# Memory attention of the first layer two steps earlier, its value products in the banks of the turned tiles, filler products given out at five rates

## The chip, the cores and the metric

The kernel runs on one core of a Trainium2 chip. TensorE (PE in the profile; its weight loads are PEld) multiplies matrices into PSUM, which holds eight banks of 128 rows by 512 float32. ScalarE (ACT), VectorE (DVE) and GpSimd (POOL) do the rest, and SyncE (SP) issues most transfers. The metric is the device time of one execution in microseconds (us), and less is better. Every engine works through its own list of instructions in the order in which the program gives them, and an instruction that must wait for another engine waits on a semaphore.

## The reference

One batch of 512 tokens of width 1024 goes through two layers. The first layer mixes tokens by differential attention (six heads, each with two maps of 64 columns), the second by gated linear attention. In every layer, in parallel with that, four heads of cross-attention read 256 memory tokens. A gated MLP with a causal convolution follows. What matters here is the first layer:

```python
proj = h @ w_in_diff[j]                 # queries, keys, values of 6 heads; queries of the memory attention
mix = diff_attention(q, k, v, ...)      # 6 heads x 4 blocks of 128 queries, softmax of two maps, p0 - lam * p1
...
# memory_cross_attention(mem_q, mem, mem_norm[i], w_mem_kv[i], mem_qk_norm[i])
kv = rms_norm(mem, mem_norm_g) @ w_kv
logits = jnp.einsum('bqhd,bkhd->bhqk', q, k)
p = jax.nn.softmax(logits, axis=-1)
o = jnp.einsum('bhqk,bkhd->bqhd', p, v)
...
x = x + jnp.concatenate([mix, cross], axis=-1) @ w_out[i]
```

## The kernel before

Large products are done in split precision: each operand is a high part (rounded to fp32r) and a low part, and three matmuls of 128x512 stand for one product (hi·hi, hi·lo, lo·hi). A block of weights comes by DMA as `raw`; `split_weights` makes `whi` on ACT (line 201) and `wlo` on DVE (line 204). `whi` and `wlo` have five buffers each (`WB`), so a new cast waits until TensorE has used the block that lay in its buffer.

The order on TensorE is the order in which the program is written (its schedule is manual). ACT, DVE, POOL and SP are ordered by a planner that works with its own estimates of durations. So moving a TensorE step also changes the order of the other engines' lists around it.

`diff_layer` is a loop of 28 steps, t = 0 to 27. Unit u = 0 to 23 is head u // 4, block u % 4. Step t does, in this order:

1. `logits(t)`: scores of unit t into two banks of the pair `lg` (line 604); DVE adds the bias and takes the row bound (line 609), ACT takes the exponentials (line 612), and DVE combines the two maps (lines 615 to 618).
2. `values(t-2)`: the value products of unit t-2 into the head's bank of the pair `sm` (line 640). At a head's last block ACT squares (line 645), and DVE scales the result out of the bank as `o` (line 649).
3. a first share of filler, `F.fill(f)`.
4. now and then norms, and `keys0()` at one step: the memory keys are transposed and scaled into `kmT` (line 473).
5. `turn(t-1)`: unit t-1's weights are transposed into a bank of the pair `tp` (line 170) and copied out by ACT (line 629).
6. the memory attention's part of the step, with m = t - M0: `ma.turn(m-1)` (bank of `tp`; copied out by DVE for even numbers and by ACT for odd ones, line 524), `ma.values` at m = 3, 5, 7, 9 (line 537, bank of `sm`), `ma.logits` at m = 0, 2, 4, 6 (line 504, banks of `lg`; DVE line 507, ACT line 511).
7. a second share of filler.
8. `prepare` of two heads at t = 7, 8, 15, 16 (queries and keys of the head transposed into two banks of `tp` and scaled by ACT, line 580), and `finish` of a head at t = 7, 11, 15 and so on (`o` transposed into a bank of `tp`, split by ACT line 238 and DVE line 239).

Each of the pairs `mm`, `sm`, `lg`, `tp` has two banks; together they are all eight. A bank is written again when the engine that reads it has finished.

The filler (class `Filler`) is a queue of product pieces: the second and third heads' projections, memory keys and values of both layers, and from step 16 the output projection. A piece of 512 columns is six matmuls; it is entered at 1.296 us. `F.fill(us)` adds credit and gives out pieces until the credit is used; an overdraft is carried on. `F.need(name)` gives out everything up to a mark.

The profile's times belong to steps like this: TensorE starts `logits` of step 5 at 82.97 us, of 6 at 90.67, 8 at 109.17, 12 at 147.31, 13 at 156.53, 15 at 173.56, 16 at 181.82, 17 at 190.43, 18 at 197.39, 22 at 217.60.

Of the kernel before, what the change touches and what calls it, by code (L numbers as in the profile page):

```python
# [30 lines left out]
HALVES = (6, 5)  # L31
XS = 36
WB = 5
STEPS, FILL = (14, 20, 26), (2.9, 1.2, 0.8, 1.3)
K8 = tuple(range(KT))
C4 = tuple(range(4))

# [92 lines left out]
def trunk(ctx, tc, head_d, x_t, mem_t, wpack, cols_a_d, cols_d, conv_d, gate_d, rel_bias, diff_lambda, consts, onehot, out):  # L130
# [12 lines left out]
    def bank(tag):  # L143
        return ps.tile([128, 512], F32, name=f"ps_{tag}", tag=tag)
# [4 lines left out]
    def split_tiles(pool=None, tag="xs", bufs=XS):  # L149
        pool = pool or xs  # L150
        return (pool.tile([128, S], F32R, name=tag + "h", tag=tag, bufs=bufs),
                pool.tile([128, S], F32R, name=tag + "l", tag=tag, bufs=bufs))
# [4 lines left out]
    def blk(b, w=128):  # L157
        return slice(w * b, w * b + w)
# [78 lines left out]
    def split(hi, lo, src, gain):  # L237
        A.activation(hi, src, AF.Copy, scale=gain)
        V.scalar_tensor_tensor(lo, src, gain, hi.bitcast(F32), op0=ALU.mult, op1=ALU.subtract)  # L239
# [4 lines left out]
    def gemm(sh, sl, nb, key, w, evac, hook=None):  # L244
        got, open_ = [], {}

        def unit(b, k0, k1):
            if not got:
                got.extend(weights(key))
            if k0 == 0:  # L250
                open_[b] = bank("mm")[:, :w]
            p = open_[b]
            for k in range(k0, k1):
                hi, lo = got[k]
                mm(p, sh[k][:, blk(b)], hi, start=k == 0, stop=False)  # L255
                mm(p, sh[k][:, blk(b)], lo, start=False, stop=False)  # L256
                mm(p, sl[k][:, blk(b)], hi, start=False, stop=k == KT - 1)  # L257
            if k1 == KT:
                if hook is not None and b == 0:
                    hook()  # L260
                evac(b, open_.pop(b))
        for b in range(nb):
            for k in range(0, KT, 2):
                F.add(6 * w / 2370.0, lambda b=b, k=k: unit(b, k, k + 2))
# [183 lines left out]
    def mem_kv(l):  # L448
        hs, ls = [None] * KT, [None] * KT
        km = [None]  # L450

        def operands():
            if l == 0:
                mem_squares()
            km[0] = xtile().rearrange("p (b n) -> p b n", b=2)
            for k in range(KT):
                if k % 2 == 0:
                    mh, ml = split_tiles()
                c = blk(k % 2, 256)
                hs[k], ls[k] = mh[:, c], ml[:, c]  # L460
                split(hs[k], ls[k], memT[k // 2][:, c], c_mem(l, k))

        def ev(b, p):
            A.activation(km[0][:, b], p[:, :256], AF.Copy, scale=r_mem[:, b:b + 1])
            A.activation(vm[l][:, b], p[:, 256:], AF.Copy, scale=r_mem[:, b:b + 1])

        def keys():
            F.need(f"kv{l}")
            p = bank("lg")
            for hp in range(2):  # L470
                for b in range(2):
                    transpose(p[:, 256 * hp + 128 * b:256 * hp + 128 * b + 128], km[0][:, b, blk(hp)])
            A.activation(kmT[l].rearrange("p a b -> p (a b)"), p, AF.Copy, scale=c_mk(l))
        gemm(hs, ls, 2, ("kv", l), 512, ev,
             (lambda: token_rsqrt("lg", mem_acc[0], 2, r_mem)) if l == 0 else None)
        F.add(0.0, lambda: group_norm(None, km[0], 2, 4, 64))
        F.mark(f"kv{l}")
        return operands, keys


    class MemAttn:
# [46 lines left out]
        def values(self, b):  # L528
            if b == 0:
                for hp in range(2):  # L530
                    self.mix[6 + hp] = split_tiles()
            pT = self.live.pop(2 * b), self.live.pop(2 * b + 1)
            po = bank("sm")
            for hp in range(2):
                for kb in range(2):
                    for j in range(2):
                        mm(po[blk(j, 64), blk(hp)], vm[self.l][:, kb, blk(2 * hp + j, 64)],
                           pT[j][:, blk(2 * hp + kb)], start=kb == 0, stop=kb == 1)
            for hp in range(2):
                mh, ml = self.mix[6 + hp]  # L540
                split(mh[:, blk(b)], ml[:, blk(b)], po[:, blk(hp)], 1.0)
# [3 lines left out]
    def diff_layer(pool, mix, acc):  # L545
# [14 lines left out]
        def project_qk(pr):  # L560
            qk[pr] = (pool.tile([128, NB, 256], F32, name="qs", bufs=1),
                      pool.tile([128, NB, 256], F32, name="ks", bufs=1))
            gemm(xh, xl, NB, ("qk", pr), 512, halves(*qk[pr]))
            F.mark(f"qk{pr}")
# [3 lines left out]
        def norms(pr, i):  # L568
            F.need(f"qk{pr}")
            group_norm(pool, qk[pr][i], NB, 4, 64)  # L570
# [51 lines left out]
        def turn(u):  # L622
            i = u % 4
            nk = 128 * (i + 1)
            pt = bank("tp")
            for kb in range(i + 1):
                transpose(pt[:, blk(kb)], live[u][:, blk(kb)])
            wT = xtile()
            A.copy(wT[:, :nk], pt[:, :nk])
            live[u] = wT  # L630
# [40 lines left out]
        F.fill(1.2)  # L671
        prepare(1)
        ma = MemAttn(pool, 0, qm, mix, False)
        M0 = 10
        for t in range(28):
            if t == 0:
                project_qk(1)
                ops0, keys0 = mem_kv(0)
                gemm(xh, xl, NB, ("v", 1), 512, lambda b, p: A.activation(
                    v12[:, b], p, AF.Copy, scale=r[:, b:b + 1]))  # L680
                F.mark("v1")
                project_qk(2)
            if t == 2:
                ops0()
                ma.norm()
            if t == 12:
                ops1, keys1 = mem_kv(1)
                ops1()
            if t == 22:
                keys1()  # L690
            if t == 16:
                load_x(x_t)
                out_proj(0, mix, 0, None)
            if t == 26:
                rest = out_proj(0, mix, 1, acc, 5)
            f = FILL[bisect(STEPS, t)]
            m = t - M0
            if t < 24:
                logits(t)
            if 0 <= t - 2 < 24:  # L700
                values(t - 2)
            F.fill(f)
            if t in (5, 6, 13, 14):
                norms((t + 3) // 8, (t + 3) % 8)
            if t == 9:
                keys0()
            if 0 <= t - 1 < 24:
                turn(t - 1)
            if 1 <= m < 9:
                ma.turn(m - 1)  # L710
            if m in (3, 5, 7, 9):
                ma.values(m // 2 - 1)
            if m in (0, 2, 4, 6):
                ma.logits(m // 2)
            if t == 27:
                F.flush()
            F.fill(f)
            if t == 4:
                ma.queries()
            if t in (7, 8, 15, 16):  # L720
                prepare(2 * (t // 7) + (t + 1) % 8)
            if t % 4 == 3 and t >= 7:
                finish(t // 4 - 1)
# [248 lines left out]
    def load_x(src):  # L972
        for k in range(KT):
            xT[k] = xtile()
            nc.sync.dma_start(xT[k], src[k])
# [10 lines left out]
    def out_proj(l, mix, part, acc, late=None):  # L986
        got, kk = {}, dict(PASS[l][part])
        turns = cycle(("mm", "mm", "sm", "sm") if late is not None else ("mm", "sm") if acc else ("mm",))

        def unit(n, i):  # L990
            c, ks = n // 2, kk[n // 2]
            if i == 0:
                if c not in got:
                    got[c] = weights(("o", l, part, c))
                got["p", n] = bank(next(turns))
            p = got["p", n]
            product(p, got[c], n % 2, [mix[k] for k in ks], (i,))
            if i == len(ks) - 1:
                update(n, p, None if acc is None else (lambda k: c_ffn(l, k)), acc)

        def give(units):
            for u in units:
                F.add(0.65, lambda u=u: unit(*u))
        units = [(2 * c + n, i) for c, ks in PASS[l][part] for n in range(2) for i in range(len(ks))]
        if late is None:
            return give(units)
        early = [u for u in units if u[0] < 4 and kk[u[0] // 2][u[1]] != late]
        give([u for u in early if u[0] < 3])
        return lambda: give([u for u in early if u[0] == 3] + [u for u in units if u not in early])
# [158 lines left out]
```

## Time and profile before

| what | value |
|---|---|
| median of 3 runs | 1196.5 us (1195.61 to 1196.85) |
| the profiled execution | 1194.47 us |
| its span | 1192.7 us |
| TensorE busy | 1179.3 us (99%) |
| VectorE busy | 760.1 us (64%) |
| ScalarE busy | 548.3 us (46%) |
| GpSimd busy | 4.5 us |
| mean transfer rate | 99 GB/s |

TensorE is nearly always busy, so time can be won or lost only in the gaps between its instructions, or by giving it more or fewer of them. Its matmuls overlap: a 128x512 matmul is shown with about 0.39 us, but the next starts 0.23 us later. In a row of the timeline the first number is the start, the second the duration, and brackets show the idle time before it with what ended it.

### The profile page before, as it was taken

To read this page: it belongs to the slowest core of one execution; us is meant where nothing else is said; L and a number is where in the kernel's file an instruction comes from. 1 tells how busy PE (TensorE), PEld (TensorE's weight loads), DVE (VectorE), ACT (ScalarE), POOL (GpSimd) and SP (SyncE) were. 2 spreads that over 40 slices of the span, in tenths; PEclk is the share of its full clock that TensorE was granted. 3 is DMA by queue.
4 is the path that set the end of the run, shared out by engine and by line. 5 is a ranking of instruction groups with operands and counts; after the bars stand their busy time and mean duration, and the time that the engine had idled before them with its cause. 6 is when DMAs were issued, how large, how long until landed. Compare 5 with 4: busy or idle time off the path is not lost.

```text
span 1192.7 us, 14774 instructions
## 1 busy us (share of the span) xinstructions
PE 1179.3 (99%) x5656; PEld 965.8 (81%) x5656; DVE 760.1 (64%) x1270; ACT 548.3 (46%) x966; POOL 4.5 (0%) x25
## 2 busy tenths in 40 slices
PE   9999998999999999999999999999999999999998
PEld 6887776788888888888888788987888888888887
DVE  7566587687767434767556746768777743476741
ACT  6676586564434223434436534436443422243420
POOL 0000000000000000000000000000000000000000
PEclk9999999999999999999999999999999999999999
DMA  8322214042322332322342221333233233242231
GB/s 296 124 96 81 80 55 141 27 136 76 116 96 86 109 107 71 123 71 89 117 144 78 72 71 58 103 104 125 73 109 103 81 114 106 71 124 72 89 115 44
DMA packets 39268, 117.81 MB, mean 99 GB/s; under 512 B 4671, under 2 KB 6520, under 8 KB 39198
## 3 DMA queue, kind: packets, MB, share of 16 engines
q1 hardware_dynamic: 39054, 116.62, 30.5%
q8 instruction: 44, 0.72, 0.3%
q10 hardware_dynamic: 144, 0.26, 0.1%
q14 instruction: 26, 0.21, 0.1%
HBM read 112.65 MB, written 4.21 MB: 98 GB/s over the span
## 4 chain that ended last, share of the span: by engine, by line
PE 93%; DVE 3%; ACT 2%; DMA 1%; issue 1%; SPq 0%; ACTq 0%; DVEq 0%
PE ps_mm L273 8%; PE ps_mm L274 8%; PE ps_mm L272 8%; PE ps_sm L274 7%; PE ps_sm L273 7%; PE ps_sm L272 7%; PE ps_mm L255 5%; PE ps_mm L257 5%; PE ps_mm L256 5%; PE ps_lg L273 3%; PE ps_lg L272 3%; PE ps_lg L274 3%; PE ps_tp L272 3%; PE ps_tp L273 3%; PE ps_tp L274 3%; PE ps_tp L170 2%
## 5 line engine op out<-in xcount | busy, mean ns | idle before, releaser
L201 ACT CAST whi<-raw 128x1024 fp32r<-128x1024 f32 (+4 forms) x212 | 208.5, 985 | 263.9 <-PE ps_tp L273 134.7
L204 DVE TENSOR_TENSOR wlo<-raw,whi 128x1024 fp32r<-128x1024 f32 (+4 forms) x212 | 241.3, 1140 | 117.1 <-ACT whi L201 116.4
L272 PE MATMUL ps_mm<-xsh,whi 128*128 128x512 f32 x446 | 176.4, 396 | 0.0
L273 PE MATMUL ps_mm<-xsl,whi 128*128 128x512 f32 x446 | 173.8, 390 | 0.2 <-DVE xsl L239 0.2
L274 PE MATMUL ps_mm<-xsh,wlo 128*128 128x512 f32 x446 | 173.7, 389 | 0.0
L272 PE MATMUL ps_sm<-xsh,whi 128*128 128x512 f32 x386 | 150.3, 389 | 0.0
L274 PE MATMUL ps_sm<-xsh,wlo 128*128 128x512 f32 x386 | 150.2, 389 | 0.0
L273 PE MATMUL ps_sm<-xsl,whi 128*128 128x512 f32 x386 | 150.2, 389 | 0.0
L255 PE MATMUL ps_mm<-whi,xsh 128*128 128x512 f32 (+2 forms) x352 | 136.9, 389 | 0.1
L257 PE MATMUL ps_mm<-whi,xsl 128*128 128x512 f32 (+2 forms) x352 | 131.1, 373 | 0.3 <-DVE xsl L239 0.3
L256 PE MATMUL ps_mm<-wlo,xsh 128*128 128x512 f32 (+2 forms) x352 | 130.6, 371 | 0.0
L1028 ACT ACTIVATE cvo<-u,cv 128x512 f32<-128x512 f32 x88 | 71.6, 814 | 121.4 <-DVE u L1026 121.4
L273 PEld LDWEIGHTS ps_mm<-xsl,whi 128*128 128x128 f32 x446 | 83.8, 188 | 17.8 <-DVE xsl L239 0.6
L272 PEld LDWEIGHTS ps_mm<-xsh,whi 128*128 128x128 f32 x446 | 83.8, 188 | 17.5 <-issue 0.8
L274 PEld LDWEIGHTS ps_mm<-xsh,wlo 128*128 128x128 f32 x446 | 83.7, 188 | 17.4
L1029 DVE SCALAR_TENSOR_TENSOR cvo<-u,cv,cvo 128x512 f32<-128x512 f32 x88 | 65.8, 748 | 38.7 <-ACT cvo L1028 38.7
L273 PEld LDWEIGHTS ps_sm<-xsl,whi 128*128 128x128 f32 x386 | 72.5, 188 | 15.1
L272 PEld LDWEIGHTS ps_sm<-xsh,whi 128*128 128x128 f32 x386 | 72.5, 188 | 15.0
L274 PEld LDWEIGHTS ps_sm<-xsh,wlo 128*128 128x128 f32 x386 | 72.5, 188 | 15.0
L255 PEld LDWEIGHTS ps_mm<-whi,xsh 128*128 128x128 f32 x352 | 66.3, 188 | 13.8 <-issue 3.4
L257 PEld LDWEIGHTS ps_mm<-whi,xsl 128*128 128x128 f32 x352 | 66.1, 188 | 12.6 <-DVE xsl L239 0.5
L256 PEld LDWEIGHTS ps_mm<-wlo,xsh 128*128 128x128 f32 x352 | 66.4, 189 | 9.7
(257 smaller groups left out, 1734.9 us busy)
## 6 DMA issues: line engine op xcount, KB each, us to landing
raw<-in_wpack_dram SPq DMA_DIRECT2D x178, 512.0 KB, 3.5
xt<-in_x_t_dram SPq DMA_DIRECT2D x15, 256.0 KB, 5.9
raw<-in_wpack_dram SPq DMA_DIRECT2D x15, 256.0 KB, 2.6
raw<-in_wpack_dram SPq DMA_DIRECT2D x8, 384.0 KB, 3.4
xres<-xt SPq DMA_DIRECT2D x8, 256.0 KB, 2.0
xt<-xres SPq DMA_DIRECT2D x8, 256.0 KB, 3.9
out_dram<-xt SPq DMA_DIRECT2D x8, 256.0 KB, 2.0
bt<-bias_d SPq DMA_DIRECT2D x6, 256.0 KB, 3.1
```

What stands on the lines that cost most here:

```text
L170: nc.tensor.transpose(dst, src, ident[:n, :n])
L201: ins = A.copy(hi[:, c], raw[:, c])
L204: V.tensor_sub(lo[:, c], raw[:, c], hi[:, c].bitcast(F32))
L255: mm(p, sh[k][:, blk(b)], hi, start=k == 0, stop=False)
L256: mm(p, sh[k][:, blk(b)], lo, start=False, stop=False)
L257: mm(p, sl[k][:, blk(b)], hi, start=False, stop=k == KT - 1)
L272: mm(p, hi[:, blk(n)], bh, start=i == first, stop=False)
L273: mm(p, hi[:, blk(n)], bl, start=False, stop=False)
L274: mm(p, lo[:, blk(n)], bh, start=False, stop=i == last)
L1028: A.activation(c, u[:, 2:], AF.Identity, scale=cv[l][:, 2, j:j + 1], bias=cv[l][:, 3, j:j + 1])
L1029: V.scalar_tensor_tensor(c, u[:, 1:S + 1], cv[l][:, 1, j:j + 1], c, op0=ALU.mult, op1=ALU.add)
```

## The change

- `M0` goes from 10 to 8: all four `ma.logits`, the eight `ma.turn` and the four `ma.values` of the first layer are issued two steps earlier (steps 8 to 17 where they were in 10 to 19).
- `keys0()` moves from the middle of step 9 to the end of step 7.
- In the first layer `ma.values` writes a bank of the pair `tp` where it wrote one of `sm`.
- The four split tiles of the memory attention's result (`mix[6]`, `mix[7]`) come from a pool of their own with four buffers, where they took four of the 36 buffers `xs`.
- The filler's credits are five where they were four: 3.2 us for steps 0 to 7, 2.5 for 8 to 13, and then 1.2, 0.8 and 1.3 as before; it was 2.9 for steps 0 to 13.

```diff
-STEPS, FILL = (14, 20, 26), (2.9, 1.2, 0.8, 1.3)
+STEPS, FILL = (8, 14, 20, 26), (3.2, 2.5, 1.2, 0.8, 1.3)
...
         def values(self, b):
             if b == 0:
                 for hp in range(2):
-                    self.mix[6 + hp] = split_tiles()
+                    self.mix[6 + hp] = split_tiles() if self.l else split_tiles(self.pool, "mx", 4)
             pT = self.live.pop(2 * b), self.live.pop(2 * b + 1)
-            po = bank("sm")
+            po = bank("sm" if self.l else "tp")
...
-        M0 = 10
+        M0 = 8
...
             F.fill(f)
             if t in (5, 6, 13, 14):
                 norms((t + 3) // 8, (t + 3) % 8)
-            if t == 9:
-                keys0()
             if 0 <= t - 1 < 24:
                 turn(t - 1)
...
             F.fill(f)
             if t == 4:
                 ma.queries()
+            if t == 7:
+                keys0()
             if t in (7, 8, 15, 16):
                 prepare(2 * (t // 7) + (t + 1) % 8)
```

The number of instructions is the same. In the changed program TensorE's list differs from step 1 to step 19, in the order of the filler pieces and of the memory attention, and in tile names in the output projection; the lists of ACT and DVE are reordered by the planner between steps 1 and 20. GpSimd's list is the same. On SP's queue one weight load of 512 KB is issued ahead of a bias load instead of behind it.

## The prediction

> **What bounds the kernel now.** First the head of the page, then the busy time in stretches of 10 us (columns: stretch; busy us and instructions of PE, PEld, DVE, ACT, POOL; granted clock; share and rate of the DMA).
>
> ```profile
> span 1192.7 us, 14774 instructions
> PE 1179.3 (99%) x5656; PEld 965.8 (81%) x5656; DVE 760.1 (64%) x1270; ACT 548.3 (46%) x966; POOL 4.5 (0%) x25
> ```
>
> ```profile
> 110.00:120.00 10.00, 10.00 (x62) 8.42 (x61) 3.05 (x14) 4.91 (x15) 0.00 (x0) 1.00 0.01 2
> ...
> 170.00:180.00 10.00, 9.10 (x63) 6.52 (x62) 9.17 (x27) 7.96 (x24) 0.00 (x0) 1.00 0.10 33
> 180.00:190.00 10.00, 8.31 (x54) 6.48 (x53) 5.63 (x15) 5.67 (x16) 0.14 (x1) 1.00 0.76 265
> 190.00:200.00 10.00, 8.09 (x62) 6.14 (x60) 7.85 (x23) 8.82 (x32) 0.00 (x0) 1.00 0.21 67
> ```
>
> TensorE is the bound, at full clock. The change adds no instruction, so it can only open or close gaps on TensorE. They lie in steps 15 to 18 (170 to 200 us), where filler is scarce; at 110 us TensorE has none and DVE is two thirds idle. Next, who TensorE waited for in steps 5 to 25 (us in total, times, longest), and the timeline rows of the waits that matter.
>
> ```profile
> PE ps_sm L640 <- DVE o L649: 2.2, 1, 2.2
> PE ps_lg L504 <- DVE nmd L609: 1.3, 1, 1.3
> PE ps_lg L604 <- ACT xt L511: 1.1, 3, 0.5
> ...
> PE ps_lg L604 <- ACT kmT L473: 0.4, 1, 0.4
> ```
>
> ```profile
> 60.37 0.39 PE L256 MATMUL ps_mm<-wlo,xsh 128*128 128x512 f32 x1
> 60.60 0.40 PE L257 MATMUL ps_mm<-whi,xsl 128*128 128x512 f32 x1
> ...
> 90.67 1.61 PE L604 MATMUL ps_lg<-kT,qT 64*128 64x192 f32 x8
> ...
> 126.45 0.92 PE L604 MATMUL ps_lg<-kT,qT 64*128 64x192 f32 x8
> ...
> 162.54 0.71 PE L170 MATMUL ps_tp<-C,xt 128*128 128x128 f32 x5
> 163.18 1.09 PE L537 MATMUL ps_sm<-xt,vm 128*64 128x128 f32 x16
> ...
> 178.62 1.09 PE L537 MATMUL ps_sm<-xt,vm 128*64 128x128 f32 x16
> 179.64 0.55 PE L170 MATMUL ps_tp<-C,qs 128*128 128x128 f32 x3
> 180.13 0.60 PE L170 MATMUL ps_tp<-C,ks 128*128 128x128 f32 x4
> 181.08 0.66 PE L170 MATMUL ps_tp<-C,o 128*128 128x128 f32 x4 [0.34 <-ACT qT L580]
> ...
> 186.70 1.34 PE L504 MATMUL ps_lg<-kmT,xt 64*128 64x256 f32 x8 [1.26 <-DVE nmd L609]
> ...
> 200.53 0.46 PE L640 MATMUL ps_sm<-v,xt 128*128 128x128 f32 x2 [2.22 <-DVE o L649]
> ```
>
> The reader is to see four things. A filler matmul costs 0.23 us (60.37 to 60.60). At step 18 head 4 waits 2.22 us for a bank of `sm` that head 3's `o` still holds, because a memory value product holds the other. At step 16 the fourth memory logits wait 1.26 us for `lg`. And at step 6 a wait hides in a busy row: eight rows take 1.61 us where the same eight take 0.92 at step 10, so 0.69.
>
> Then ACT and DVE around steps 6, 13, 15 and 16:
>
> ```profile
> 88.71 0.29 ACT L629 COPY xt<-ps_tp 128x128 f32<-128x128 f32 x1
> ...
> 95.79 1.05 ACT L201 CAST whi<-raw 128x1024 fp32r<-128x1024 f32 x1
> ...
> 163.14 0.45 ACT L556 ACTIVATE qs<-ps_mm,r_x 128x256 f32<-128x256 f32 x1
> 163.50 0.46 ACT L557 ACTIVATE ks<-ps_mm,r_x 128x256 f32<-128x256 f32 x1
> 163.86 0.62 ACT L308 ACTIVATE xt<-qs 128x512 f32<-128x512 f32 x1
> 164.38 0.25 ACT L629 COPY xt<-ps_tp 128x128 f32<-128x128 f32 x1
> ...
> 178.33 0.46 ACT L629 COPY xt<-ps_tp 128x384 f32<-128x384 f32 x1
> ...
> 180.34 0.69 ACT L580 ACTIVATE qT<-ps_tp,cols 128x512 f32<-128x512 f32 x1 [0.30 <-PE ps_tp L170]
> ...
> 184.60 0.84 ACT L201 CAST whi<-raw 128x768 fp32r<-128x768 f32 x1 [2.15 <-PE ps_mm L257]
> 185.34 0.58 ACT L629 COPY xt<-ps_tp 128x512 f32<-128x512 f32 x1
> 186.68 0.40 ACT L612 ACTIVATE xt<-xt,nmd 128x128 f32<-128x128 f32 x1 [0.76 <-DVE nmd L609]
> ...
> 187.47 0.56 ACT L524 COPY xt<-ps_tp 128x512 f32<-128x512 f32 x1
> ```
>
> ```profile
> 185.48 0.96 DVE L204 TENSOR_TENSOR wlo<-raw,whi 128x768 fp32r<-128x768 f32 x1 [2.24 <-ACT whi L201]
> 186.35 0.28 DVE L609 CUSTOM_DVE_ANT_0 xt<-ps_lg,bt 128x128 f32<-128x128 f32 x1
> ```
>
> A cast of weights (184.60) stands idle for 2.15 us until TensorE has used up the block in its buffer, and everything behind it in ACT's list stands too: the copy of the turned weights at 185.34, and through DVE's line 204 the row bounds at 186.35. Lags: ACT starts 0.15 us after TensorE's last transpose (179.64 + 0.55 to 180.34), TensorE 0.05 after ACT's end (180.34 + 0.69 to 181.08).
>
> **The change part by part.** I walked the changed program's four lists and put these durations on them. Where a number is a bound I say so.
>
> *Value products leave `sm` (gain).* Only heads use `sm` then, head 4 gets the bank that head 2 freed at step 12, and its first product waits only for its own copied weights, long done. Gain 2.22; if the copy were late, 0.
>
> *No memory logits at step 16 (gain).* The 1.26 at step 16 goes, with 0.22 at step 17 (the rest of the 1.1 of line 511; 0.9 lies at step 15 and stays, since memory logits still stand at step 14 ahead of the same two filler pieces). But that work was also cover; see step 16.
>
> *Memory attention from step 8.* The analogue of 0.22 now falls at step 9, where two pieces and eight transposes stand between memory logits and the next scores: +0.2, between 0 and 0.5. `keys0` ahead of `prepare` puts one ACT scaling in front of the head's: +0.15, between 0 and 0.4. No filler is removed, and DVE has room there (3.05 of 10 at 110 us), so steps 8, 10 and 12 cost nothing more; if that cover is gone it is 0.5 a step.
>
> *Credits.* 16 shares of 3.2 and 12 of 2.5 are 81.2 us, as 28 of 2.9 are: no filler is gained or lost, but pieces come earlier. At step 6 this moves the copy of unit 4's weights. It ran at 88.71, ahead of three casts; now it stands behind three casts and two squares. From the transpose: six matmuls until the first buffer is free, 1.4; the memory norm ahead of it, 0.5 (estimate); three casts at 0.95 (1.05 each, the next starting 0.1 before the end), 2.85; a key evacuation 0.36, two squares at 0.52, the copy 0.25, lags 0.2: 6.6. TensorE has 18 matmuls and one set of scores, 4.15 + 0.95 = 5.1. Wait 1.5, against 0.69 that goes since the memory norm now has 18 matmuls of cover: +0.8, between -0.7 (the copy in time) and +1.3.
>
> *Value products enter `tp` (loss).* Each follows at once behind `turn` and `ma.turn`, which hold both banks, so it waits for ACT's copy of `turn`. Steps 11 and 15: the copy of three blocks ends at 178.79 while the product started at 178.62: +0.3 each, between 0 and 0.7. Step 17 has no `ma.turn`: 0. Step 13: the copy stands behind the last piece's evacuation. From that piece's end: 0.15, lines 556 and 557 0.72, two squares 1.04, two small operations 0.3 (estimate), the copy 0.25, 0.05: 2.5, and TensorE arrives after 0.64 (162.54 to 163.18). Wait 1.9; the lower bound is the old run's own copy, 164.63 + 0.05 - 163.18 = 1.5; the upper 2.4, if a cast is late by half its length.
>
> *Step 15, behind the product.* `qs`, `ks` and `o` follow with the product's bank still held by its splits, so all three pass through one bank. `ks` waits for the scaling of `qs`: 0.15 + 0.69 + 0.05 = 0.9; `o` for the product's last low part: 0.3 (estimate); the old 0.34 goes. +0.85, between 0 and 1.4.
>
> [...]
>
> *Step 16 (loss).* ACT's list holds two casts of 768 columns ahead of the copy of unit 15's weights. The second waits for the last filler matmul, and right behind that matmul TensorE wants the copy's bank for `qs`. Wait 0.15 + 0.74 (184.60 to 185.34) + 0.58 + 0.05 = 1.5. `ks` then wants the bank of `ma.turn`, copied by line 524, which stands where it did at 187.47, behind the cast, line 204, the row bounds and two exponentials: 184.60 to 188.03 is 3.43 after the cast's start, so 3.63 after the filler; less 1.5 and 0.49 of `qs`, 1.6. Together 3.1, between 0.8 (cast done early, one copy left) and 3.9. In the old order memory logits stood between.
>
> *The rest.* The four tiles leave `xs`: no instruction, nothing that waited for `xs` on TensorE: 0. Their memory is used again by the MLP's `u`, whose clearing now waits until nearly the end of the output projection:
>
> ```profile
> POOL u L1015 <- PE ps_tp L170: 200.2, 2, 140.7
> ```
>
> It had 140 us of slack; the first convolution comes over 24 matmuls (5.5 us) after, so 0; without this cover a clearing of under 1 us. On SP one weight load passes a bias load; it is issued a step ahead: 0, at worst the load's landing of 3.1 us. The 0.4 at step 22 stays.
>
> ```profile
> bt<-bias_d SPq DMA_DIRECT2D x6, 256.0 KB, 3.1
> ```
>
> Sum: -2.22 - 1.26 - 0.22 + 0.2 + 0.15 + 0.8 + 0.3 + 0.3 + 1.9 + 0.85 + 3.1 = +3.9. The profiled execution took 1194.47 us, 2.0 below the median, and would be 1198.4; the median 1196.5 becomes 1200.4.
>
> **The rivals.** *ACT comes in time (faster).* If ACT reaches the copies of steps 13 and 16 within 0.64 us of their transposes, 1.9 and 3.1 shrink to 0.3 and 0; the wait of step 6 must shrink too. 3.9 - 1.6 - 3.1 - 1.5 = -2.3, and with step 15's line down to 0, -3.2: 1193.3. For it: ACT is idle by half over the span. Against: at step 16 the cast is tied to TensorE's own last matmul, and no idle time beforehand helps. It decides if the cast stands ahead of that filler on the chip.
>
> *Waits feed on each other (no change).* Each wait lets ACT and DVE catch up, so that one of the two large ones fades: 3.9 - 1.9 = +2.0, 1198.5. For it: DVE and ACT are busy 9.17 and 7.96 of 10 at 170 us, so backlog is real. Against: the two waits hang on instructions issued just before, not on backlog.
>
> *The clock falls (slower still).* Step 16 would hold TensorE for 3.1 us with 0.49 between. If the clock were halved for as long, half of it is lost again: 1202. The stretch with 2.22 idle shows 1.00, so there is no sign of it. [...]
>
> **How the numbers follow.** 0.2% (2.4 us) is about what a measurement of this kernel can tell from no change. The sum holds: 0.70. Waits fade: 0.18. In time: 0.09. Clock: 0.03. So slower 0.73, same 0.18, faster 0.09. Predicted 1200.4. All lower ends at once give -2.1, all upper ends +7.6: 1194.4 to 1204.1. I cut the lower end at 1195.8, which leaves out most of the faster case, and keep 1204.1.
>
> **What would show it.** No wait on `o` at step 18, none of line 504 at step 16; instead line 537 waiting for line 629 at step 13, about 1.9, and `qs` and `ks` waiting for lines 629 and 524 at step 16, about 1.5 and 1.6; line 640 waiting at step 6. It is wrong if line 537 starts right behind its transposes, or if step 16's copies end before the filler.

## The result, and the profile after

The changed kernel takes 1199.72 us (median of 12 runs, 1197.45 to 1202.32), the kernel before 1195.92 us in the same comparison (median of 12, 1194.44 to 1196.85). The ratio is 1.0034, with a 95% interval of 1.0024 to 1.0043: slower, by about 0.3%. The profiled execution of the changed kernel took 1197.67 us, 3.2 more than the profiled one before.

The head of its page:

```profile
span 1195.9 us, 14770 instructions
PE 1178.8 (99%) x5656; PEld 964.5 (81%) x5656; DVE 761.1 (64%) x1270; ACT 548.3 (46%) x966; POOL 4.5 (0%) x25
```

TensorE's work is what it was (1178.8 against 1179.3 us busy), and the span is 3.2 us longer: the loss is idle time. Who TensorE waited for between 80 and 240 us (us in total, times, longest):

```profile
PE ps_tp L537 <- ACT xt L629: 2.5, 3, 2.1
PE ps_tp L170 <- ACT xt L524: 1.4, 1, 1.4
PE ps_tp L170 <- ACT xt L629: 1.4, 1, 1.4
PE ps_tp L170 <- ACT qT L580: 1.3, 2, 0.8
PE ps_sm L640 <- ACT xt L629: 1.3, 1, 1.3
...
PE ps_lg L504 <- DVE nmd L609: 0.3, 1, 0.3
PE ps_lg L604 <- ACT xt L511: 0.2, 1, 0.2
```

The 2.2 for `o` is gone and the 1.3 for `nmd` is down to 0.3. In their place stand four entries of waits for ScalarE's copies of turned tiles, lines 629 and 524. TensorE's timeline says where (start, duration, idle time before it):

```profile
97.05 0.49 PE L640 MATMUL ps_sm<-v,xt 128*128 128x128 f32 x2 [1.25 <-ACT xt L629]
...
115.34 0.66 PE L170 MATMUL ps_tp<-C,o 128*128 128x128 f32 x4 [0.48 <-ACT qT L580]
...
123.94 1.06 PE L604 MATMUL ps_lg<-kT,qT 64*128 64x128 f32 x8
...
170.15 1.09 PE L537 MATMUL ps_tp<-xt,vm 128*64 128x128 f32 x16 [2.13 <-ACT xt L629]
...
181.39 1.13 PE L604 MATMUL ps_lg<-kT,qT 64*128 64x256 f32 x6 [0.21 <-ACT xt L511]
...
185.50 1.09 PE L537 MATMUL ps_tp<-xt,vm 128*64 128x128 f32 x16 [0.18 <-ACT xt L629]
...
187.96 0.66 PE L170 MATMUL ps_tp<-C,ks 128*128 128x128 f32 x4 [0.78 <-ACT qT L580]
...
195.81 0.66 PE L170 MATMUL ps_tp<-C,qs 128*128 128x128 f32 x4 [1.41 <-ACT xt L629]
197.91 0.66 PE L170 MATMUL ps_tp<-C,ks 128*128 128x128 f32 x4 [1.44 <-ACT xt L524]
...
205.19 0.49 PE L640 MATMUL ps_sm<-v,xt 128*128 128x128 f32 x2
```

The last row is head 4's first value product, without a wait. Step 6 (97.05), step 13 (170.15) and step 16 (195.81, 197.91) pay. ScalarE's rows say why:

```profile
92.50 1.04 ACT L201 CAST whi<-raw 128x1024 fp32r<-128x1024 f32 x1
...
95.27 1.04 ACT L201 CAST whi<-raw 128x1024 fp32r<-128x1024 f32 x1
96.21 0.63 ACT L308 ACTIVATE xt<-qs 128x512 f32<-128x512 f32 x1
96.74 0.26 ACT L629 COPY xt<-ps_tp 128x128 f32<-128x128 f32 x1
...
168.34 0.47 ACT L557 ACTIVATE ks<-ps_mm,r_x 128x256 f32<-128x256 f32 x1
168.70 0.21 ACT L192 ACTIVATE rs_y<-rs_y 128x4 f32<-128x4 f32 x1
168.79 1.15 ACT L308 ACTIVATE xt<-qs 128x512 f32<-128x512 f32 x2
169.83 0.27 ACT L629 COPY xt<-ps_tp 128x128 f32<-128x128 f32 x1
...
192.18 0.83 ACT L201 CAST whi<-raw 128x768 fp32r<-128x768 f32 x1 [2.19 <-PE ps_mm L257]
194.44 0.83 ACT L201 CAST whi<-raw 128x768 fp32r<-128x768 f32 x1 [1.43 <-PE ps_mm L257]
195.18 0.58 ACT L629 COPY xt<-ps_tp 128x512 f32<-128x512 f32 x1
...
197.29 0.56 ACT L524 COPY xt<-ps_tp 128x512 f32<-128x512 f32 x1
```

A copy of 0.26 to 0.58 us stands last in a row of casts and squares. At step 16 it is worse than being last: ScalarE is idle for 2.19 and 1.43 us in front of two casts, because it takes its list in order and the casts must wait for TensorE's own filler; the finished transposes wait behind. In stretches of 10 us (columns as in the prediction):

```profile
110.00:120.00 10.00, 9.52 (x55) 7.77 (x54) 2.28 (x9) 4.10 (x9) 0.14 (x1) 1.00 0.01 4
170.00:180.00 10.00, 9.85 (x64) 7.38 (x64) 9.37 (x25) 6.03 (x19) 0.00 (x0) 1.00 0.24 83
...
190.00:200.00 10.00, 7.15 (x49) 5.72 (x49) 4.64 (x14) 5.06 (x11) 0.00 (x0) 1.00 0.87 307
```

From 190 to 200 us TensorE, VectorE and ScalarE are all less busy than before (7.15, 4.64 and 5.06 against 8.09, 7.85 and 8.82): none of the three is overloaded in this stretch.

The 12 runs fall into groups by their mean granted clock: four with 1.000 lie at 1197.45 to 1197.76 (the profiled execution is one of them), three with 0.999 at 1199.44 to 1199.89, and five with 0.995 to 0.997 at 1200.73 to 1202.32; the experiments show what this is.

### The profile page after: what moved, and what is told of

It reads as the page before. It is cut to its first block, busy times and chain, and to the rows that moved or that the text cites. A ratio compares the mean times of both kernels' runs of the same rounds, so it can differ in the third digit from the quotient of the medians.

```text
span 1195.9 us, 14770 instructions
## 1 busy us (share of the span) xinstructions
PE 1178.8 (99%) x5656; PEld 964.5 (81%) x5656; DVE 761.1 (64%) x1270; ACT 548.3 (46%) x966; POOL 4.5 (0%) x25
## 4 chain that ended last, share of the span: by engine, by line
PE 90%; ACT 4%; DVE 3%; DMA 2%; issue 1%; SPq 0%; ACTq 0%; DVEq 0%
PE ps_mm L273 8%; PE ps_mm L274 8%; PE ps_mm L272 8%; PE ps_sm L273 7%; PE ps_sm L272 7%; PE ps_sm L274 7%; PE ps_mm L255 5%; PE ps_mm L257 5%; PE ps_mm L256 5%; PE ps_lg L273 3%; PE ps_lg L272 3%; PE ps_lg L274 3%; PE ps_tp L272 3%; PE ps_tp L273 3%; PE ps_tp L274 3%; PE ps_tp L170 2%
## 5 line engine op out<-in xcount | busy, mean ns | idle before, releaser
L272 PE MATMUL ps_mm<-xsh,whi 128*128 128x512 f32 x438 | 173.3, 396 | 0.0
L273 PE MATMUL ps_mm<-xsl,whi 128*128 128x512 f32 x438 | 170.6, 390 | 0.2 <-DVE xsl L239 0.2
L274 PE MATMUL ps_mm<-xsh,wlo 128*128 128x512 f32 x438 | 170.6, 390 | 0.0
L272 PE MATMUL ps_sm<-xsh,whi 128*128 128x512 f32 x378 | 147.1, 389 | 0.0
L274 PE MATMUL ps_sm<-xsh,wlo 128*128 128x512 f32 x378 | 147.1, 389 | 0.0
L273 PE MATMUL ps_sm<-xsl,whi 128*128 128x512 f32 x378 | 147.0, 389 | 0.0
```

Of the source, the lines that this page charges most:

```text
L272: mm(p, hi[:, blk(n)], bh, start=i == first, stop=False)
L273: mm(p, hi[:, blk(n)], bl, start=False, stop=False)
L274: mm(p, lo[:, blk(n)], bh, start=False, stop=i == last)
```

## The experiments

The theory is that the loss comes from ScalarE's list: copies of `tp` banks stand behind casts of weights that needn't be there. The rivals are that the bank of the value products, the rates or the earlier memory attention as such is the cause, or that the engines are just behind. Each time below is the median of the version's runs, with the ratio to the kernel before and its interval. "Undisturbed" is the median of those of its runs whose mean clock was 1.000: 1197.70 for the changed kernel (4 runs), and 1194.9 for the kernel before (39 of the 80 runs taken beside the experiments).

**The head's preparation one step later.**

```diff
-            if t in (7, 8, 15, 16):
+            if t in (7, 8, 15):
                 prepare(2 * (t // 7) + (t + 1) % 8)
...
+            if t == 17:
+                prepare(5)
```

> The changed kernel with the preparation of the head of unit 5 moved from the end of step 16 to the end of step 17; nothing else. Theory (the copies of turned tiles stand behind two casts in ScalarE's list, and the transposes of qs and ks come right behind the filler that the second cast waits for): the two waits of step 16, 1.41 for line 629 and 1.44 for line 524, go, since at step 17 a last memory value product and the scores of the step lie between; of their 2.85 us at most 0.9 comes back as a wait for qT, line 580, at step 17, so the span is 2.0 to 2.9 us below the changed kernel's. Rival 1 (ScalarE and VectorE are simply behind here, and TensorE pays wherever it next needs them): the 2.85 comes back within two steps under another name, the span is within 0.5 us of the changed kernel's. Rival 2 (memory attention was the cover that is missing, so any place without it costs the same): the waits appear at step 17 at about 1.4 each.

Measured: 1199.33 us, 1.0028 (1.0018 to 1.0038); only two of its 8 runs were undisturbed (1197.75 and 1199.11). The two waits of step 16 went, and TensorE paid elsewhere (timeline):

```profile
198.10 0.98 PE L604 MATMUL ps_lg<-kT,qT 64*128 64x128 f32 x8 [2.12 <-DVE nmd L609]
...
206.74 0.63 PE L170 MATMUL ps_tp<-C,ks 128*128 128x128 f32 x4 [0.51 <-DVE rs_v L184]
```

2.12 + 0.51 = 2.63 in place of 2.85: the first rival held, and the theory in this form fell. It isn't the place of the transposes. The casts still stand idle, for 2.19 and 1.41 us, now with the row bounds of the next scores behind them.

This execution had a mean clock of 0.997. The granted clock in stretches of 0.25 us shows why:

```profile
171.25:171.50 0.25, 0.25 (x3) 0.25 (x2) 0.25 (x2) 0.14 (x1) 0.00 (x0) 1.00 0.23 86
171.50:171.75 0.25, 0.25 (x2) 0.20 (x2) 0.25 (x2) 0.25 (x2) 0.00 (x0) 0.57 0.03 12
171.75:172.00 0.25, 0.25 (x3) 0.15 (x2) 0.25 (x1) 0.22 (x2) 0.00 (x0) 0.50 0.00 0
...
174.75:175.00 0.25, 0.25 (x2) 0.16 (x2) 0.14 (x1) 0.00 (x0) 0.00 (x0) 0.61 0.60 197
...
198.75:199.00 0.25, 0.25 (x4) 0.08 (x1) 0.14 (x1) 0.25 (x3) 0.00 (x0) 0.68 1.09 184
...
202.25:202.50 0.25, 0.25 (x3) 0.21 (x2) 0.00 (x0) 0.25 (x3) 0.00 (x0) 0.99 0.00 0
```

Twice the clock was at 0.50: from 171.54 to 174.95 (0.57 is 1.00 for 0.04 us and 0.50 for the rest) and from 198.84 to 202.26, so 3.41 us each time. The first began 1.35 us after the 2.13 of step 13 had ended (170.19 in this run), the second 0.74 us after the 2.12. Half of 3.41 is lost each time, and that accounts for the span: 1195.9 - 0.22 + 2 x 1.7 = 1199.1, as measured.

**The value products in `sm` again.**

```diff
-            po = bank("sm" if self.l else "tp")
+            po = bank("sm")
```

> The changed kernel with the memory value products of the first layer written to the two banks of sm again; earlier memory attention and five rates stay. Theory: the waits of line 537 (0.19, 2.13 and 0.18 at steps 11, 13 and 15) go, and with them the 0.78 of line 170 for qT at step 15, 3.3 in all; a wait of line 640 for o, line 649, comes back at step 18 at about 2.2, since the last memory value product, at step 17, then holds one of the two banks. The waits of step 16 (1.41 and 1.44) stay within 0.3. Span 1.1 us below the changed kernel's, between 0.5 and 3.3 lower. Rival 1 (the bank matters little, the products would have waited for their operands): line 537 still waits at step 13 by 1.5 or more. Rival 2 (the crowding of the banks of tp also makes the waits of step 16): those two fall by over 1 us together.

Measured: 1196.47 us, 1.0006 (0.9996 to 1.0015); undisturbed 1195.47 (5 runs). The waits of line 537 are gone, that for `qT` is back to 0.8 in two pieces (0.7 in the kernel before), and step 16 is untouched, as is the 1.25 at step 6:

```profile
PE ps_tp L170 <- ACT xt L524: 1.4, 1, 1.4
PE ps_tp L170 <- ACT xt L629: 1.4, 1, 1.4
PE ps_sm L640 <- ACT xt L629: 1.3, 1, 1.3
```

So the bank is worth 2.2 us of loss, and both rivals fell. One point of the theory fell too: the 2.2 for `o` at step 18 did not come back. In this version it can't be told whether the 2.85 at step 16 gave VectorE the time to catch up; the versions below can.

**The old four rates.**

```diff
-STEPS, FILL = (8, 14, 20, 26), (3.2, 2.5, 1.2, 0.8, 1.3)
+STEPS, FILL = (14, 20, 26), (2.9, 1.2, 0.8, 1.3)
```

> The changed kernel with the old four rates of giving out products (2.9 in every step before 14). Theory: only the order at step 6 and the filler's position hang on the rates: the wait of line 640 for line 629, 1.25, goes and about 0.7 of it hides again in the scores of step 6, so 0.6 to 0.8 us less; the waits of steps 13 and 16 (2.13, 1.41 and 1.44) stay within 0.5 each, since the casts and evacuations that stand ahead of the copies are the same. Span 0.3 to 1.3 us below the changed kernel's. Rival 1 (the rates put the casts and the last piece in front of the copies, so the rates are the whole loss): the three waits go too, span 4 or more below. Rival 2 (the rates are what keeps filler for the late steps): new waits of 1 us or more between steps 8 and 17, span higher than the changed kernel's.

Measured: 1198.39 us, 1.0019 (1.0009 to 1.0028); undisturbed 1196.91 (3 runs), 0.8 below the changed kernel. The wait of step 6 is gone, step 16 unchanged. Step 13, which the theory held fixed, fell from 2.13 to 1.44:

```profile
169.69 1.09 PE L537 MATMUL ps_tp<-xt,vm 128*64 128x128 f32 x16 [1.44 <-ACT xt L629]
```

Neither rival appeared. So the rates cost at two places: they also put the last piece's evacuation later against the transposes of step 13.

**The bank alone, in the kernel before.**

```diff
-            po = bank("sm")
+            po = bank("sm" if self.l else "tp")
```

> The kernel before with one change: the memory value products of the first layer are written to the banks of tp. Theory: the wait of line 640 for o at step 18, 2.22, goes; line 537 waits for line 629 at step 13 by 1.5 to 2.1, at steps 15, 17 and 19 by 0.2 to 0.6 each, and the three tiles qs, ks and o of step 15 go through one bank, 0.8: span between 0.5 and 2.0 us above the kernel before. The waits of step 16 for lines 629 and 524 don't appear, since memory logits still stand there. Rival 1 (the bank alone is a gain and the loss is all from the earlier memory attention and the rates): span 1 to 2.3 us below the kernel before. Rival 2 (the bank is the whole loss): span 3 us or more above it.

Measured: 1196.97 us, 1.0008 (0.9999 to 1.0017), which alone can't be told from no change; undisturbed 1196.72 (6 runs), 1.8 above the kernel before, and its profiled execution 1.6 above. The 2.22 for `o` is gone, line 537 waits 1.44 at step 13, 0.20 at step 15, and 1.24 at step 17, where 0.2 to 0.6 was expected. Neither rival held: the bank alone is a small loss, not a gain and not the whole.

**The idle casts out of ScalarE's list.** The cast of a piece is written where the piece before it begins; the planner had pulled the output weights several steps forward. Counted from 160 us, the second to fourth cast of 768 columns stand at 185.35, 192.18 and 194.44, so the idle ones are those of the third and fourth piece, not the second and third as the text below has it. The second and third are kept in program order here, and the fourth, whose buffers come after theirs, went along (line 222):

```diff
-            split_weights(slice(0, n * w), raw, hi, lo, len(made) == 2)
+            split_weights(slice(0, n * w), raw, hi, lo, len(made) in (2, 8, 9))
```

> The changed kernel with the casts of the second and third piece of output weights kept in program order (the condition of line 220 reads 2, 8, 9 in place of 2): the two casts that stood idle at step 16, at 192.18 and 194.44 us, leave ScalarE's list there and stand four steps later; nothing else. Theory (the casts that wait for TensorE's own last filler matmul are the cause of step 16): the waits of 1.41 for line 629 and 1.44 for line 524 go, at most 0.5 is left, the wait at step 13 stays at 2.1; no new wait over 0.8 in steps 16 to 20. Undisturbed span 2.0 to 2.9 us below the changed kernel's, 1193.0 to 1193.9, and fewer runs with a clock below 1.000, since one of the two places that can start a fall is gone. Rival 1 (ScalarE and VectorE are behind by then and TensorE pays anyway): 1.5 us or more of waits in steps 16 and 17 under other names. Rival 2 (the casts are needed early, and put later they make the output weights late): waits of line 272 for lines 201 or 204 of 1 us or more from step 18 on.

Measured: 1196.04 us, 1.0005 (0.9997 to 1.0014); undisturbed 1195.58 (6 runs, from 1194.8). The waits of step 16 are gone, and in their place stand 0.62 instead of 0.42 at step 22, 0.37 at step 24, and 0.28 for `kT` at step 16:

```profile
220.15 0.91 PE L604 MATMUL ps_lg<-kT,qT 64*128 64x192 f32 x6 [0.62 <-ACT kmT L473]
228.00 0.94 PE L640 MATMUL ps_sm<-v,xt 128*128 128x128 f32 x6 [0.37 <-ACT xt L629]
```

This one line is worth 2.1 us undisturbed and 3.7 us in the median. It settles step 16: moving TensorE's step gained next to nothing, while taking the casts away removed both waits and kept about three quarters of their 2.85 us.

**The value product behind the second filler.**

```diff
-            if m in (3, 5, 7, 9):
-                ma.values(m // 2 - 1)
...
             F.fill(f)
+            if m in (3, 5, 7, 9):
+                ma.values(m // 2 - 1)
```

> The changed kernel with the memory value product of a step put behind the step's second filler, ahead of the next head's preparation, in place of ahead of it; the bank stays tp. Theory (line 537 at step 13 only comes too soon behind the transposes whose copy it waits for): the wait of 2.13 at step 13 falls to below 0.5 and those of 0.19 and 0.18 go, while at step 15, which has its filler spread over the same step, qs and ks still follow behind the product and wait 0.8 to 1.6 for a bank. Undisturbed span 1.2 to 2.5 us below the changed kernel's. Rival (the bank of tp is taken until the copy in any case, so whatever comes first pays): the first to ask for tp after step 13's transposes still waits 1.5 or more, and the span stays within 0.5 us.

Measured: 1197.86 us, 1.0018 (1.001 to 1.0027); undisturbed 1196.96 (4 runs), 0.7 below the changed kernel where 1.2 to 2.5 was expected. The 2.13 is gone, but `tp` has two banks and the next to ask pays 0.81; and the scores of step 15 wait 0.33 and 0.52 for line 511, where they waited 0.29 and 0.21:

```profile
175.81 0.63 PE L170 MATMUL ps_tp<-C,xt 128*128 128x128 f32 x4 [0.81 <-DVE mxl L239]
...
180.63 1.13 PE L604 MATMUL ps_lg<-kT,qT 64*128 64x256 f32 x6 [0.52 <-ACT xt L511]
```

Theory and rival were each half right.

**Only the earlier memory attention and its tiles:** `sm` and the old rates, so both diffs above at once.

> Only the earlier memory attention and its own tiles of the change: the value products stay in sm and the old four rates stay. Theory: the waits of step 16 (1.41 and 1.44) are there in full, those of line 537 at steps 11 to 15 and of line 640 at step 6 are not, and that of line 640 for o at step 18 is not either, since with memory attention two steps sooner the last value product meets a freed bank, as in the run with sm alone. From the kernel before: +2.85 at step 16, -2.22 at step 18, -1.26 and -0.22 of memory logits, +0.2 at step 9, +0.15 at step 8: -0.5, so an undisturbed span of 1192.2, between 1191.5 and 1193.5. Rival (bank and rates hid something): a wait of 1 us or more for o or for line 629 comes back, span 1194 or more.

Measured: 1196.55 us, 1.0002 (0.9993 to 1.001); undisturbed 1194.58 (4 runs), 0.3 below the kernel before. The waits are as expected, 1.41 and 1.44 at step 16 and none for `o`. Against the changed kernel it gains 3.1, the sum of the 2.2 of the bank and the 0.8 of the rates. But 7 of its 12 runs had a clock below 0.9985, the profiled one too (0.62 from 196 to 200 us), and in the median nothing is left of the gain.

**The same, with the casts in program order.**

> The version before with the casts of the second and third piece of output weights kept in program order as well: earlier memory attention, values in sm, old rates, no cast that stands idle at step 16. Theory: what is left are waits below 1 us, in all 3 us or less between 60 and 245 us; undisturbed span 1189.5 to 1191.0, so 1.5 to 3 us below the kernel before, and the runs stand close together (within 1.5 us) with a clock of 1.000 in nearly all, since no wait of over 1 us is left that could pull the clock down. Rival 1 (the clock falls by itself now and then): runs with a clock of 0.999 and less stay as frequent as in the kernel before. Rival 2 (the casts come too late): waits of line 272, span no lower than that of the version without the kept order.

Measured: 1192.42 us (5 runs, 1191.84 to 1192.85), 0.9969 (0.9957 to 0.9981), all at a clock of 1.000. This beats both kernels. What is left to wait for between 60 and 245 us adds up to 3.4, a little over the 3 expected, and no single wait is above 0.6:

```profile
PE ps_lg L604 <- ACT xt L511: 0.9, 2, 0.5
PE ps_tp L170 <- ACT qT L580: 0.8, 2, 0.5
...
PE ps_sm L640 <- DVE o L649: 0.3, 1, 0.3
```

With `sm`, and without the pause at step 16, the wait for `o` at step 18 is 0.3. So the bank was not needed to remove the 2.22.

**The kernel before, with the casts in program order.**

> The kernel before with the casts of the second and third piece of output weights kept in program order, and nothing of the change. Theory (one idle cast stands behind the wait of line 504 at step 16, the bank of o behind that of line 640 at step 18, and the two are separate): the 1.26 for nmd goes or falls below 0.4, the 2.22 for o at step 18 stays at 1.5 or more; undisturbed span 0.9 to 1.5 us below the kernel before. The earlier memory attention is then worth what this version lacks against the version with everything, about 2 us. Rival 1 (the idle cast is behind both waits): the 2.22 falls below 0.5 too, the span comes within 0.6 us of the best version's 1190.6, and the earlier memory attention is worth nothing. Rival 2 (memory logits at step 16 hide the casts): nothing moves by 0.4 us.

Measured: 1194.24 us, 0.9987 (0.9978 to 0.9996). The first rival held: the 1.26 and the 2.22 are both gone, and the profiled span of 1191.1 is 0.5 above the best version's. A new wait stands at step 22, and ScalarE's list shows its cause:

```profile
PE ps_lg L604 <- ACT kmT L473: 1.7, 1, 1.7
```

```profile
212.50 1.05 ACT L201 CAST whi<-raw 128x1024 fp32r<-128x1024 f32 x1 [1.35 <-DMA raw<-in_wpack_dram]
```

So the casts stood behind both large waits of the kernel before; which of the three that moved was not separated. The cure has a price of the same kind: a cast at 212.50 us stands idle for weights that have not landed yet, and ScalarE works without a pause from there to the end of `kmT` at 216.86, just before TensorE goes on. Against the best version the earlier memory attention is worth 0.5 us in the profiled spans and 0.2 among undisturbed runs (1192.61, only 2 of 11, against 1192.42); the 1.8 in the median goes with the granted clock, which is below 1.000 in the other nine.

**The five rates in the best version.**

> The best version so far with the change's five rates put back in place of the old four; nothing else. Theory (rates alone move the copy of unit 4's weights behind three casts, and nothing else of weight): the wait of line 640 for line 629 at step 6 is there at 1.2 to 1.3, about 0.4 of line 312's wait at step 7 goes, no other wait grows by over 0.3; span 0.6 to 1.2 us above the best version's 1190.6. A wait of 1.25 alone starts no fall of the clock: all runs at 1.000. Rival (the rates help once the casts are out of the way): span within 0.3 us of the best version's, or below it.

Measured: 1193.2 us, 0.9979 (0.997 to 0.9988), profiled span 1191.3, 0.7 above the best version. The 1.25 at step 6 is there, as expected. Three runs had a clock of 0.999, where 1.000 was expected, but at 1193.09 to 1194.31 they are no longer than the rest. In the profiled one every stretch of 4 us from 60 to 244 us shows 1.00; the clock falls at 1189.86 us, after TensorE's last matmul (1187.24), and costs nothing. So a mean clock of 0.999 alone does not prove a loss.

## Why the prediction was right, and where not

The predicted median was 1200.4 and the measured one is 1199.72; the predicted change of the profiled execution was +3.9 and the measured one +3.2. By the steps of the sum:

- **`sm` freed, -2.22:** the wait went. But the bank was not needed for it: the casts that ScalarE took early made `o` late, and without them the wait goes in `sm` too (0.3 in the best version, none in the kernel before with the casts in order). With the memory attention two steps earlier it goes in `sm` even with those casts.
- **Memory logits out of step 16, -1.26 and -0.22:** gone. A new 0.29 for the same `nmd` at step 12 was not in the sum.
- **Steps 8 and 9, +0.15 and +0.2:** 0.14 (0.48 against 0.34) and 0.35 (eight rows of scores take 1.06 where 0.71 is usual).
- **Step 6, +0.8:** 1.25 less the hidden 0.69, so 0.56. The run with the old rates shows that the rates are the cause.
- **Steps 11 and 15, +0.3 each:** 0.19 and 0.18.
- **Step 13, +1.9:** 2.13. I gave it all to the bank; the bank makes 1.44 of it, and the rates the other 0.7.
- **Step 15, +0.85:** `ks` 0.78 for 0.9 and nothing for `o`, where I had 0.3; less the old 0.34, 0.44. Line 511's 0.9, which I left standing, is 0.21; the other wait there, 0.29, is now for VectorE's line 179, so 0.5 in all.
- **Step 16, +3.1:** 1.41 and 1.44, 2.85, by the mechanism named, the second cast tied to the last filler matmul.
- **Tiles, GpSimd, SP, at nothing:** no wait for any of them appeared.

The measured terms add up to -3.70 + 0.29 + 0.14 + 0.35 + 0.56 + 0.37 + 2.13 + 0.44 - 0.41 + 2.85 = 3.0, of the 3.2 measured. My 0.9 too much is mostly line 511, which I held fixed, `o` at step 15, which did not wait, and step 16.

The range's upper end was worked out wrongly: "all upper ends +7.6" counts the 2.22 of `sm` as gained, though its own bound was 0. With that bound it is +9.8. The result does not depend on it.

That the median came out so close was in part luck. I carried the 2.0 us between the profiled execution and the median as a constant that I did not understand. It goes with the falls of the clock, in both kernels: undisturbed the change costs 2.8 us (1197.70 against 1194.9) and in the profiled executions 3.2, in the median 3.8. So between 0.6 and 1 us of the median's loss goes with the clock, and that made up for a sum that was 0.7 too high. The rival "the clock falls", at 0.03 and 1202, is therefore not refuted: three of the twelve runs lie at 1202.03 to 1202.32. The fall happens in some executions and not in others; "the stretch with 2.22 idle shows 1.00, so there is no sign of it" was the failed step, since it took one execution for all. The two other rivals fell: ScalarE did not come in time, and no large wait faded.

## What to carry to other kernels

When a copy out of PSUM is late, look at what stands ahead of it in its engine's list, and whether that is idle: here a cast that had no hurry waited in order for TensorE, and one changed condition was worth 2.1 us in the median of the kernel before, 3.7 in the changed one and 4.1 with earlier memory attention alone. Both times that the waiting step was moved instead, some or nearly all of the wait came back elsewhere. A cast put later must still not stand in front of weights that land late: that cost up to 1.35 us at step 22. Before an offset between one profiled execution and the median is carried along, look at what the other runs did, their granted clock above all.

## What the runs showed of the hardware

In some executions TensorE's granted clock fell to 0.50 for a stretch. In the run with the preparation moved, both falls last 3.41 us and begin 27.30 us apart, 8.0 times 3.41. Five profiled executions show six falls between 168 and 204 us, each behind a wait of step 13 or 16 or, with the preparation moved, step 17. The changed kernel's own profiled execution has the same 2.13 and shows none there: its clock is 1.00 in every stretch of 4 us from 60 to 244 us.

Where the waits lie may explain this. In both kernels and in the run with the preparation moved the record shows one more fall near its end, when TensorE has finished; in the kernel before the clock is 0.91 from 1193.00 to 1193.25 us and 0.50 after that, and its last matmul starts at 1188.55. With the preparation moved this fall begins at 1198.95 us (the mean clock from 1180 to 1200 is 0.97), 1027.41 us after the one at 171.54; an eighth of 27.30 goes into that about 301 times, which is 3.4133 us a step. If falls begin only at such steps, which is an estimate of mine from these three starts, the steps can be laid out backwards from the last fall of an execution. The rows show the stretch between two steps (start and end in us, its length, then TensorE's busy time; the clock is the third figure from the end): first the changed kernel, a stretch at step 13 and the start of the last fall (1195.96); then the run with the preparation moved, the two stretches ahead of its falls.

```profile
168.55:171.96 3.41, 1.81 (x19) 1.53 (x20) 2.92 (x8) 2.89 (x9) 0.00 (x0) 1.00 0.69 228
1195.75:1196.00 0.25, 0.00 (x0) 0.00 (x0) 0.00 (x0) 0.00 (x0) 0.00 (x0) 0.93 0.00 0
```

```profile
168.12:171.53 3.41, 1.34 (x17) 1.15 (x18) 2.91 (x10) 2.92 (x9) 0.00 (x0) 1.00 0.76 254
195.43:198.84 3.41, 1.29 (x11) 0.86 (x9) 1.55 (x6) 2.08 (x6) 0.00 (x0) 1.00 0.89 321
```

In the changed kernel an edge at 168.55 cuts the 2.13 into 0.53 and 1.60, and one at 195.86 parts the 1.41 of step 16 from the 1.44, so no stretch between 60 and 245 us holds more than 1.60 us of idle time. In the other run one stretch holds 2.07 and one 2.12. The 3.41 us ahead of the six falls held 1.57 to 2.75 us of idle time. In the kernel before, laid out in the same way, the most is 1.61, from 196.51 to 199.92, where an edge cuts the 2.22 as well, and no fall followed. The other five profiled executions have a clock of 1.00 in every stretch of 4 us from 60 to 244 us. My estimate from these numbers is that a fall followed where some 1.6 us of such a stretch were idle, and that the place of a wait among the steps decided whether it filled one that far. The two values overlap by 0.04 us, and no run moved a wait against the steps, so neither is shown.

The price agrees with the runs: half of 3.41 is 1.7 us, and the changed kernel's times stand at 1197.6, 1199.6 and about 1201.5. The kernel before has its runs with less than 1.000 at 1196.7, 1.8 above the others, so it probably pays for such falls too, in 41 of 80 runs (five of the other 39 lie at 1196.0 to 1196.8 all the same, and why is open); the best version, without a wait of over 0.6 us there, has a clock of 1.000 in all 5. No run of the kernel before with such a clock was profiled, so where its falls lie is not shown, and the same holds for the kernel before with the casts in order, whose largest wait is 1.75.
